# Strassen's algorithm for 28 of the 32 K tiles of each MLP's second product, with its sums on VectorE

## The chip, the core and the metric

One core of one Trainium2 chip runs the whole kernel. The metric is the device time of one execution in microseconds (us), as the median of several runs. The engines are TensorE (PE in the profile; PEld is its loading of the stationary operand), VectorE (DVE), ScalarE (ACT), GpSimd (POOL) and SyncE (SP), which only issues transfers here.

## The reference

A trunk of two layers works on 512 tokens of width 1024, in float32. Each layer has a token mixer (differential attention in layer 0, a short gated convolution in layer 1) and an MLP of width 4096, each between two RMS norms and added to the residual:

```python
def sq_relu_mlp(h, x, w_up, w_down):
    return jnp.square(jax.nn.relu(x @ w_up)) @ w_down

for i in range(DEPTH):                                   # DEPTH = 2
    h = rmsnorm(x, norm_mixer_pre[i])
    m = diff_attention(h, ...) if i % 2 == 0 else short_conv(h, ...)
    x = x + rmsnorm(m, norm_mixer_post[i])
    h = rmsnorm(x, norm_mlp_pre[i])
    x = x + rmsnorm(sq_relu_mlp(h, mlp_w_up[i], mlp_w_down[i]), norm_mlp_post[i])
```

The change concerns the product with `w_down`: [512 tokens, 4096] times [4096, 1024], in both layers.

## The kernel before

Every float32 operand is split into two parts, `hi` (rounded) and `lo` (the rest), and a product of two operands is three matmuls into one PSUM bank: `mm3`, lines 63 to 65. A bank holds 128 x 512 numbers.

**Weights.** A unit of weights is [128, 1024]: one K tile of `w_down` (`dn`) with all 1024 output columns, or one tile of 128 features of `w_up` (`up`) with its 8 K tiles. SP loads the raw unit (three buffers). ACT casts `hi` (line 143) and DVE subtracts to get `lo` (line 144), in `split_to`; `use` has the units split three ahead of the one in use, and 9 units have room as parts.

**The MLP.** `mlp_steps` says in which order groups of up tiles and groups of K tiles ("dn") follow each other. An up tile makes 128 hidden features for all 512 tokens: 24 matmuls of 512 columns into one bank (`feature_tiles`). The first six up tiles of a layer are an exception (`HALVED`): they go in two passes of 256 tokens, 24 matmuls of 256 columns per tile and pass, since the first tokens are normed and transposed before the last. ACT then takes relu and square out of the bank (lines 569, 570), and DVE makes the two parts of the activations, `u_hi` and `u_lo` (lines 572, 573).

`down(g)` multiplies a group of K tiles: groups of 4, 4, 4, 4, 4, 4 and 8. For each block of 128 tokens and each half of the output columns, the K tiles of the group run up in one bank, and DVE adds the bank into `acc` in SBUF (line 606; line 604 copies in the first group). The banks take turns over six. The four up tiles of a group lie between two such groups on PE. The last group of 8 goes by whole token blocks. Behind each block comes `block_end`: the post norm (`mg`, line 501; the mean square on ACT; the power -1/2 on POOL, line 70), the residual (`x_sb`, line 506), the next norm (`hn`, line 515). `turn` transposes `hn` on PE through banks 6 and 7 (line 523), and ACT and DVE take the parts out (`hT_hi`, line 526, `hT_lo`, line 527). It is put behind 18 further steps of PE (`after`, `step`); a step is one `mm3` of 512 columns. What comes next is the convolution's first product (`ci`), whose first tiles go in two passes of 256 tokens as well.

Each engine runs its instructions in order. The order is made once, when the program is built, by a scheduler that takes for each engine what its model thinks is ready.

Of the kernel before, what the change touches and what calls it, by code (L numbers as in the profile page):

```python
# [16 lines left out]
P = 128  # L17
T = 512
# [9 lines left out]
DOWN_GROUPS = (4, 4, 4, 4, 4, 4, 8)  # L28
MASKED = -3.0e38
SLOTS = 9  # L30
# [3 lines left out]
SHARERS = {2: {30, 31}, 4: {29}}  # units of attention that are last to use the banks  # L34
# [3 lines left out]
def trunk(ctx: ExitStack, tc: tile.TileContext, x, xT, w_qk, w_v, w_o, w_in, w_out,  # L38
# [6 lines left out]
    up_ = ctx.enter_context(tc.tile_pool(name="u", bufs=9))  # L45
# [41 lines left out]
    # ---- weights: units of [P, 1024] in the order of their use, loaded as slots fall free and  # L87
    # ---- split exactly into two parts of 12 bits some units ahead of their use
    starts = [sum(DOWN_GROUPS[:g]) for g in range(len(DOWN_GROUPS))]
    group = [list(range(s, s + n)) for s, n in zip(starts, DOWN_GROUPS)]  # L90
    conv_order = [8, 16, 0, 9, 17, 1] + [r * KT + ct for ct in range(2, KT) for r in (1, 2, 0)]
    order = [("v", k, w_v[k]) for k in range(KT)]
    order += [(n, h, w_qk[2 * h + i]) for h in range(H) for i, n in enumerate("qk")]
    order += [("wo", k, w_o[k]) for k in range(KT)]

    # the last group of K tiles goes through whole token blocks, the others through all tokens at once
    mlp_steps = [("up", 0)]
    for g in range(len(group) - 1):
# [12 lines left out]
    raws, units, xts = [], [], []
    n_done = [0]

    def issue():
        while len(raws) < min(len(order), len(units) + RAWS):
            n, i, src = order[len(raws)]
# [12 lines left out]
            raws.append(raw)  # L129
# [4 lines left out]
    def split_to(j):  # L134
        for j_ in range(len(units), min(j + 1, len(order), n_done[0] + SLOTS)):
            n, i, _ = order[j_]
            raw = raws[j_]
            if n == "v":
                split_xT(i)
            hi = wp.tile([P, 1024], F32R, tag="whi", name=f"hi_{n}_{i}")  # L140
            lo = wp.tile([P, 1024], F32R, tag="wlo", name=f"lo_{n}_{i}")
            for s in pieces(1024, j_ < 2 or n in "qk"):
                (DVE.tensor_copy if j_ < 1 else ACT.copy)(hi[:, s], raw[:, s])  # L143
                DVE.tensor_tensor(lo[:, s], raw[:, s], hi[:, s].bitcast(F32), op=ALU.subtract)  # L144
            units.append((hi, lo))
# [23 lines left out]
    def split_xT(kt):  # L169
        """x transposed (as laid out by the host), times the gain"""  # L170
# [14 lines left out]
    ones = const.tile([P, P], F32, name="ones")  # L185
# [6 lines left out]
    mask = const.tile([P, P], F32, name="mask")  # L192
# [73 lines left out]
    def rotate(i, which, h, p):  # L266
# [9 lines left out]
        def split_q(c, mine, other):  # L276
            """scaled: hi and lo of each component, where its rows are"""
# [4 lines left out]
        def twin_q(c, mine, other):  # L282
            """hi again, on the other half of the rows"""
# [432 lines left out]
```

## Time and profile before

| | |
|---|---|
| median of 3 runs | 1155.06 us (1154.93 to 1156.70) |
| profiled execution, first to last instruction (span) | 1153.8 us |
| PE busy | 1134.4 us, 98% of the span, 5584 matmuls |
| DVE busy | 632.9 us, 55% |
| ACT busy | 434.5 us, 38% |
| POOL busy | 100.3 us, 9% |

The profiled execution has no time of its own besides its span; the median of the runs is 1.3 us longer than that span. A busy share is a mean over the program, so the sections below look at stretches of it. The MLP of layer 0 lies at about 262 to 615 us, the convolution at 615 to 800, the MLP of layer 1 behind that.

### The profile page before, as it was taken

Reading aid. Unit: us, or ns where it says so; the run is one execution under the profiler, and the core shown is the slowest. Engines: PE = TensorE matmul, PEld = TensorE weight load, DVE = VectorE, ACT = ScalarE, POOL = GpSimd, SP = SyncE. Lnnn points to the kernel's source line nnn. Section 1 sums busy time; section 2 is a strip of 40 time slices with the busy share of each in tenths; the row PEclk is TensorE's granted clock in tenths of the full one; section 3 lists DMA queues with packets and bytes.
Section 4 is the critical chain, followed back from the end, with each engine's and each line's share of the span. In section 5 each row is a group of like instructions: output and inputs, shape, how many; then the busy total and the mean of one; then the engine's idle time right before and its main releaser. Section 6 shows DMA issues by size and latency. Waiting matters only on the chain.

```text
span 1153.8 us, 14203 instructions
## 1 busy us (share of the span) xinstructions
PE 1134.4 (98%) x5584; PEld 946.8 (82%) x5584; DVE 632.9 (55%) x1007; ACT 434.5 (38%) x789; POOL 100.3 (9%) x108
## 2 busy tenths in 40 slices
PE   9999999999999999999999999999999999999997
PEld 7867677779888888888889988889988888888886
DVE  6589999666543443544357544447544434434424
ACT  6546666544422322313324432225423223222411
POOL 0144454211000000000001000000000000000000
PEclk9999999999999999999999999999999999999999
DMA  8611111044431421423205323303414314313201
GB/s 317 217 59 52 56 56 55 19 152 153 134 103 43 146 99 48 146 74 128 92 1 183 129 91 99 102 19 130 144 37 146 106 40 146 100 46 130 89 19 55
DMA packets 33044, 114.32 MB, mean 99 GB/s; under 512 B 3793, under 2 KB 4433, under 8 KB 32977
## 3 DMA queue, kind: packets, MB, share of 16 engines
q1 hardware_dynamic: 32976, 113.41, 29.3%
q8 instruction: 44, 0.72, 0.3%
q14 instruction: 24, 0.19, 0.1%
HBM read 111.30 MB, written 2.10 MB: 98 GB/s over the span
## 4 chain that ended last, share of the span: by engine, by line
PE 83%; DVE 11%; POOL 3%; issue 2%; ACT 1%; DMA 0%; SPq 0%; POOLq 0%; DVEq 0%; ACTq 0%
PE bank L63 25%; PE bank L65 25%; PE bank L64 25%; PE pair L206 2%; PE bank L206 2%; DVE nm L372 1%; DVE a L397 1%; POOL t_q L272 1%; PE bank L523 1%; DVE k L289 1%; DVE pair L371 1%; PE pair L63 1%; PE pair L65 1%; PE pair L64 1%; DVE q L284 1%
## 5 line engine op out<-in xcount | busy, mean ns | idle before, releaser
L63 PE MATMUL bank<-hT_hi,hi_up 128*128 128x512 f32 (+1 forms) x608 | 216.5, 356 | 0.0
L64 PE MATMUL bank<-hT_lo,hi_up 128*128 128x512 f32 (+1 forms) x608 | 216.3, 356 | 0.0
L65 PE MATMUL bank<-hT_hi,lo_up 128*128 128x512 f32 (+1 forms) x608 | 216.2, 356 | 0.0
L63 PE MATMUL bank<-hi_dn,u_hi 128*128 128x512 f32 (+1 forms) x520 | 200.8, 386 | 0.0
L65 PE MATMUL bank<-hi_dn,u_lo 128*128 128x512 f32 (+1 forms) x520 | 200.6, 386 | 0.0
L64 PE MATMUL bank<-lo_dn,u_hi 128*128 128x512 f32 (+1 forms) x520 | 200.6, 386 | 0.0
L143 ACT CAST hi_dn<-raw_dn 128x1024 fp32r<-128x1024 f32 x64 | 65.8, 1053 | 245.8 <-PE bank L65 141.9
L606 DVE TENSOR_TENSOR acc<-bank,acc 128x512 f32<-128x512 f32 (+1 forms) x97 | 66.2, 684 | 149.5 <-PE bank L65 149.5
L144 DVE TENSOR_TENSOR lo_dn<-raw_dn,hi_dn 128x1024 fp32r<-128x1024 f32 x64 | 77.6, 1223 | 104.9 <-ACT hi_dn L143 104.9
L65 PEld LDWEIGHTS bank<-hT_hi,lo_up 128*128 128x128 f32 x608 | 114.7, 189 | 16.2
L64 PEld LDWEIGHTS bank<-hT_lo,hi_up 128*128 128x128 f32 x608 | 114.8, 189 | 16.2
L63 PEld LDWEIGHTS bank<-hT_hi,hi_up 128*128 128x128 f32 x608 | 114.7, 189 | 16.2
L143 ACT CAST hi_up<-raw_up 128x1024 fp32r<-128x1024 f32 x64 | 66.4, 1051 | 157.5 <-PE bank L65 65.9
L144 DVE TENSOR_TENSOR lo_up<-raw_up,hi_up 128x1024 fp32r<-128x1024 f32 x64 | 77.8, 1223 | 72.8 <-ACT hi_up L143 72.8
L63 PEld LDWEIGHTS bank<-hi_dn,u_hi 128*128 128x128 f32 x520 | 97.7, 188 | 19.7
L64 PEld LDWEIGHTS bank<-lo_dn,u_hi 128*128 128x128 f32 x520 | 97.7, 188 | 19.6
L65 PEld LDWEIGHTS bank<-hi_dn,u_lo 128*128 128x128 f32 x520 | 97.7, 188 | 19.6
L63 PE MATMUL bank<-hT_hi,hi_ci 128*128 128x512 f32 (+1 forms) x240 | 83.4, 347 | 0.0
L64 PE MATMUL bank<-hT_lo,hi_ci 128*128 128x512 f32 (+1 forms) x240 | 83.2, 347 | 0.0
L65 PE MATMUL bank<-hT_hi,lo_ci 128*128 128x512 f32 (+1 forms) x240 | 83.2, 347 | 0.0
L64 PEld LDWEIGHTS bank<-hT_lo,hi_ci 128*128 128x128 f32 x240 | 45.4, 189 | 5.7
L65 PEld LDWEIGHTS bank<-hT_hi,lo_ci 128*128 128x128 f32 x240 | 45.4, 189 | 5.7
(195 smaller groups left out, 1652.9 us busy)
## 6 DMA issues: line engine op xcount, KB each, us to landing
raw_up<-in_w_up SPq DMA_DIRECT2D x64, 512.0 KB, 3.5
raw_dn<-in_w_down SPq DMA_DIRECT2D x64, 512.0 KB, 3.5
raw_ci<-in_w_in SPq DMA_DIRECT2D x24, 512.0 KB, 3.4
raw_q<-in_w_qk SPq DMA_DIRECT2D x8, 512.0 KB, 4.3
raw_k<-in_w_qk SPq DMA_DIRECT2D x8, 512.0 KB, 4.3
raw_wo<-in_w_o SPq DMA_DIRECT2D x8, 512.0 KB, 3.5
raw_wc<-in_w_out SPq DMA_DIRECT2D x8, 512.0 KB, 3.4
raw_v<-in_w_v SPq DMA_DIRECT2D x7, 512.0 KB, 5.1
```

The source lines that it names most:

```text
L63: PE.matmul(o, lhsT=a[0], rhs=b[0], start=start, stop=False)
L64: PE.matmul(o, lhsT=a[0], rhs=b[1], start=False, stop=False)
L65: PE.matmul(o, lhsT=a[1], rhs=b[0], start=False, stop=stop)
L143: (DVE.tensor_copy if j_ < 1 else ACT.copy)(hi[:, s], raw[:, s])
L144: DVE.tensor_tensor(lo[:, s], raw[:, s], hi[:, s].bitcast(F32), op=ALU.subtract)
L206: PE.matmul(banks[2 * b + n], lhsT=hT[ai][:, kt, b * P:(b + 1) * P], rhs=w[bi][:, n * 512:(n + 1) * 512], start=kt == 0 and ai + bi == 0, ...
L272: POOL.tensor_tensor(t1, t1, sw, op=ALU.add)
L284: DVE.tensor_scalar(tiles[c][other], t1[mine], HD ** -0.5, None, op0=ALU.mult)
L289: DVE.tensor_tensor(tiles[c][other], t1[mine], tiles[c][mine].bitcast(F32), op=ALU.subtract)
L371: DVE.tensor_tensor(dgl, dgl, mask.unsqueeze(1).broadcast_to([P, 2, P]), op=ALU.add)
L372: DVE.tensor_reduce(nm, s[:, :, :w], axis=AX.X, op=ALU.max, negate=True)
L606: DVE.tensor_tensor(a, o, a, op=ALU.add)
```

## The change

28 of the 32 K tiles of each layer's second product go in 14 pairs. A pair is a 2 x 2 block problem: two K tiles by two halves of the tokens (256 each) on the side of the activations, two K tiles by two halves of the columns (512 each) on the side of the weights. Instead of the 8 products of such blocks there are 7, of sums of blocks. Two pairs make a group, so there are 7 groups per layer. A product of a group is 12 matmuls: two pairs by two token blocks by three.

- **Activations.** Relu and square of the two tiles of a pair go into one scratch tile `F` of eight blocks [128, 256], of which there is one buffer. DVE makes four sums of blocks in three instructions; `ua` (768 wide) and `ub` (1024 wide) are split into parts, `hi` now on ACT. The scratch of the norms (`jk`) and of the convolution uses `F` too.
- **Weights.** A pair's raw weights are one tile of five blocks of 512 (`rawd`, two buffers), and its units are `A` (1024, split as loaded), `E` (sums of 1024 and 512, then split), `D` (512 per pair) and `G` (a sum of 512, then split). Units are split four ahead, into 6 slots; in the other stages two more lie in the buffers of `rawd`.
- **Products.** X is banks 0 and 1, Y is 2 and 3, Z is 4 and 5. In order: X, Y, X again (it runs on in the same bank), Z, X, Z, X. After each of the seven DVE adds both banks into a quarter of `acc` (`into`); in the first group the first write of each quarter is an ACT copy. Up tiles behind the first six use banks 6 and 7 in turn.
- **Order.** Four up tiles lie between two groups, six before the last. The four K tiles that are left go by token blocks as before (`tail`); `turn` follows after 14 steps, and `mg` has two buffers instead of three.

```diff
-DOWN_GROUPS = (4, 4, 4, 4, 4, 4, 8)
-SLOTS = 9
+PAIRED = 28
+GROUP = 2
+SLOTS = 6
+LEAD = 4
+RAWDS = 2
...
+        else:
+            r, (h2, l2) = parts[0], (t.rearrange("p (a b) -> p a b", a=2) for t in (hi, lo))
+            if n[0] == "A":
+                split(h2, l2, r[:, 0:4:2, :])
+            if n[0] == "E":
+                DVE.tensor_tensor(r[:, 0:2, :], r[:, 0:2, :], r[:, 1:4:2, :], op=ALU.add)
+                DVE.tensor_tensor(r[:, 4, :], r[:, 0, :], r[:, 3, :], op=ALU.add)
+                split(h2, l2, r[:, 0:5:4, :])
+            if n[0] == "D":
+                for k, p in enumerate(parts):
+                    split(h2[:, k, :], l2[:, k, :], p[:, 3, :])
+            if n[0] == "G":
+                DVE.tensor_tensor(r[:, 2, :], r[:, 4, :], r[:, 2, :], op=ALU.add)
+                split(h2, l2, r[:, 1:3, :])
...
-            sq = t512(late, f"relu_{l}_{i}", "relu", 3)
-            ACT.activation(sq, o, AF.Relu)
-            ACT.activation(sq, sq, AF.Square)
-            u = u_tile(f"u_{l}_{i}")
-            DVE.tensor_copy(u[0], sq)
-            DVE.tensor_tensor(u[1], sq, u[0].bitcast(F32), op=ALU.subtract)
-            us[i] = u
...
+                held[p] = late.tile([P, 8, 256], F32, tag="F", name=f"F_{l}_{p}", bufs=1)
+            f = held[p]
+            squared(o.rearrange("p (a b) -> p a b", a=2), f[:, k:k + 3:2, :])
...
+            split(*a, f[:, 1:4, :])
+            DVE.tensor_tensor(f[:, 4:6, :], f[:, 1:3, :], f[:, 0:1, :].broadcast_to([P, 2, 256]), op=ALU.subtract)
+            DVE.scalar_tensor_tensor(f[:, 6, :], f[:, 4, :], -1.0, f[:, 2, :], op0=ALU.mult, op1=ALU.subtract)
+            DVE.scalar_tensor_tensor(f[:, 7, :], f[:, 6, :], -1.0, f[:, 3, :], op0=ALU.mult, op1=ALU.subtract)
+            split(*b, f[:, 4:8, :])
...
+        def product(g, o, first, form, kind, half):
+
+            for p in groups[g]:
+                w = use(f"{kind}{l}", p if kind != "D" else g)
+                s = half if kind != "D" else groups[g].index(p)
+                s = slice(512 * s, 512 * s + 512)
+                for t in range(2):
+                    step(lambda: mm3(o[t], part(us[form, p], ALL, slice(t * P, (t + 1) * P)), part(w, ALL, s),
+                                     first and p == groups[g][0], p == groups[g][-1], not first))
+
+        def into(c, o, op, fresh=False):
+
+            for t in range(2):
+                a = acc[:, (2 if c[0] == 1 else 0) + t, 512 * (c[1] - 1):512 * c[1]]
+                if fresh:
+                    ACT.activation(a, o[t], AF.Copy, scale=1.0 if op == ALU.add else -1.0)
+                else:
+                    DVE.tensor_tensor(a, a, o[t], op=op)
 
         def down(g):
...
+            x, y, z = ([banks[2 * i], banks[2 * i + 1]] for i in range(3))
+            new, pq = g == 0, groups[g]
+            product(g, x, True, "A11", "A", 0)
+            into((1, 1), x, ALU.add, new)
+            product(g, y, True, "A12", "A", 1)
+            into((1, 1), y, ALU.add)
...
+            product(g, x, False, "S2", "E", 1)
+            into((1, 2), x, ALU.subtract, new)
+            product(g, z, True, "S1", "E", 0)
+            into((2, 2), z, ALU.subtract, new)
...
+            product(g, x, False, "S3", "G", 0)
+            into((2, 2), x, ALU.subtract)
+            product(g, z, False, "S4", "D", 0)
+            into((1, 2), z, ALU.subtract)
+            done(f"D{l}", g)
+            product(g, x, False, "A22", "G", 1)
+            into((2, 1), x, ALU.add, new)
```

How the instructions stand on DVE before, in the second group of K tiles of layer 0 (`bank4` and `bank5` are banks that `down` has filled, `lo_dn0_9` is the second part of a unit that comes later):

```order
L573 TENSOR_TENSOR u_0_11_lo_3330<-relu_0_11_3326,u_0_11_hi_3329 128x512
L606 TENSOR_TENSOR acc_81<-bank4_2593,acc_81 128x512
L606 TENSOR_TENSOR acc_81<-bank5_2594,acc_81 128x512
...
L606 TENSOR_TENSOR acc_81<-bank4_2593,acc_81 128x512
L144 TENSOR_TENSOR lo_dn0_9_3536<-raw_dn0_9_3364,hi_dn0_9_3535 128x1024
L606 TENSOR_TENSOR acc_81<-bank5_2594,acc_81 128x512
L144 TENSOR_TENSOR lo_dn0_10_3573<-raw_dn0_10_3465,hi_dn0_10_3572 128x1024
```

And on DVE in the changed kernel, in the third group of layer 0 (pairs 4 and 5; `lo_G0_4` is the second part of unit G of pair 4, `ua_0_6` and `ub_0_6` are the activations of pair 6, which the next group uses; bank 0 at the end is the third product's):

```order
L201 TENSOR_TENSOR lo_G0_4_3578<-rawd_0_4_3329,hi_G0_4_3577 128x1024
L699 TENSOR_TENSOR F_0_6_3519<-F_0_6_3519 128x512
L724 TENSOR_TENSOR acc_81<-acc_81,bank0_70 128x512
L201 TENSOR_TENSOR ua_0_6_lo_3555<-F_0_6_3519,ua_0_6_hi_3554 128x768
L700 SCALAR_TENSOR_TENSOR F_0_6_3519<-F_0_6_3519 128x256
L724 TENSOR_TENSOR acc_81<-acc_81,bank1_71 128x512
L701 SCALAR_TENSOR_TENSOR F_0_6_3519<-F_0_6_3519 128x256
L724 TENSOR_TENSOR acc_81<-acc_81,bank2_2575 128x512
...
L201 TENSOR_TENSOR lo_G0_5_3605<-rawd_0_5_3332,hi_G0_5_3604 128x1024
L201 TENSOR_TENSOR ub_0_6_lo_3557<-F_0_6_3519,ub_0_6_hi_3556 128x1024
L201 TENSOR_TENSOR lo_up0_14_3616<-raw_up0_14_3361,hi_up0_14_3615 128x1024
L724 TENSOR_TENSOR acc_81<-acc_81,bank0_70 128x512
```

The adds of banks, which stood almost alone, now stand among sums and splits. Between the second product's add (bank 3, left out) and the third product's (bank 0) there are three splits of 1024.

On ACT at the same place of the changed kernel:

```order
L674 ACTIVATE F_0_6_3519<-bank6_72 128x2x256
L675 ACTIVATE F_0_6_3519<-F_0_6_3519 128x2x256
L200 CAST hi_G0_4_3577<-rawd_0_4_3329 128x1024
L674 ACTIVATE F_0_6_3519<-bank7_73 128x2x256
L675 ACTIVATE F_0_6_3519<-F_0_6_3519 128x2x256
L200 CAST ua_0_6_hi_3554<-F_0_6_3519 128x768
L200 CAST hi_G0_5_3604<-rawd_0_5_3332 128x1024
```

The cast of `hi_G0_4` needs a slot, and it stands ahead of the second tile's relu.

On DVE at the tail of layer 0 in the changed kernel, between the second and the third token block (`m0_1`, `m0_2`; banks 2 and 3 are block 2's, bank 4 is block 3's, banks 6 and 7 at the end hold the transposes of block 1):

```order
L621 SCALAR_TENSOR_TENSOR hn_m0_1_1_5071<-x_sb_2313,rb_m0_1_5066,g_pre2_2581 128x512
L768 TENSOR_TENSOR acc_81<-bank3_2576,acc_81 128x512
L607 TENSOR_TENSOR mg_m0_2_0_5111<-acc_81,g_post1_2579 128x512
L607 TENSOR_TENSOR mg_m0_2_1_5113<-acc_81,g_post1_2579 128x512
L601 TENSOR_SCALAR a_m0_2_0_5115<-a_m0_2_0_5115 128x1
L201 TENSOR_TENSOR lo_ci_17_5212<-raw_ci_17_4954,hi_ci_17_5211 128x1024
L73 TENSOR_SCALAR ra_m0_2_5122<-a_m0_2_1_5116,a_m0_2_0_5115 128x1
L768 TENSOR_TENSOR acc_81<-bank4_2577,acc_81 128x512
L612 SCALAR_TENSOR_TENSOR x_sb_2313<-mg_m0_2_0_5111,ra_m0_2_5122,x_sb_2313 128x512
L612 SCALAR_TENSOR_TENSOR x_sb_2313<-mg_m0_2_1_5113,ra_m0_2_5122,x_sb_2313 128x512
L633 TENSOR_TENSOR hT_lo_80<-bank6_72,hT_hi_79 128x4x128
```

The parts of block 1's transposes stand behind the residual of block 2, as before; new between them are a split of the convolution's weights and the first add of block 3.

## Rows read from the trace of the kernel before

**Rows 1.** The page, parts 1, 2 and 4: busy time, granted clock, chain

```profile
PE 1134.4 (98%) x5584; PEld 946.8 (82%) x5584; DVE 632.9 (55%) x1007; ACT 434.5 (38%) x789; POOL 100.3 (9%) x108
...
PEclk9999999999999999999999999999999999999999
...
PE 83%; DVE 11%; POOL 3%; issue 2%; ACT 1%; DMA 0%; SPq 0%; POOLq 0%; DVEq 0%; ACTq 0%
```

**Rows 2.** Windows: stretch, PE, PEld, DVE, ACT, POOL busy, granted clock, DMA share

```profile
230.00:262.00 32.00, 30.05 (x150) 24.71 (x149) 20.48 (x40) 15.28 (x35) 5.05 (x6) 1.00 0.46 153
...
288.00:420.00 132.00, 132.00 (x624) 111.00 (x623) 61.76 (x80) 42.22 (x55) 0.00 (x0) 1.00 0.30 96
...
570.00:615.00 45.00, 45.00 (x208) 37.41 (x207) 25.86 (x46) 16.16 (x35) 4.34 (x8) 1.00 0.08 26
```

**Rows 3.** Groups by form, PE: busy, mean ns of one, idle before

```profile
L63 PE MATMUL bank<-hi_dn,u_hi 128*128 128x512 f32 x504 | 196.2, 389 | 0.0
```

**Rows 4.** Timeline of PE: the second product, 24 matmuls from start to start

```profile
570.02 0.39 PE L63 MATMUL bank<-hi_dn,u_hi 128*128 128x512 f32 x1
...
575.46 0.39 PE L63 MATMUL bank<-hi_dn,u_hi 128*128 128x512 f32 x1
```

**Rows 5.** Timeline of PE: matmuls of 256 columns, start to start

```profile
290.07 0.28 PE L63 MATMUL bank<-hT_hi,hi_up 128*128 128x256 f32 x1
...
290.43 0.28 PE L63 MATMUL bank<-hT_hi,hi_up 128*128 128x256 f32 x1
```

**Rows 6.** Groups by form, DVE

```profile
L144 DVE TENSOR_TENSOR lo_dn<-raw_dn,hi_dn 128x1024 fp32r<-128x1024 f32 x64 | 77.6, 1223 | 104.9 <-ACT hi_dn L143 104.9
L606 DVE TENSOR_TENSOR acc<-bank,acc 128x512 f32<-128x512 f32 x95 | 65.4, 690 | 146.7 <-PE bank L65 146.7
L573 DVE TENSOR_TENSOR u_lo<-relu,u_hi 128x512 fp32r<-128x512 f32 x64 | 44.3, 693 | 2.2
L572 DVE CAST u_hi<-relu 128x512 fp32r<-128x512 f32 x64 | 27.4, 427 | 3.6 <-ACT relu L570 3.6
...
L397 DVE SCALAR_TENSOR_TENSOR a<-p,rho 128x256 f32<-128x256 f32 x8 | 3.8, 476 | 0.0
```

**Rows 7.** Timeline of DVE: instructions one behind the other

```profile
503.98 1.23 DVE L144 TENSOR_TENSOR lo_up<-raw_up,hi_up 128x1024 fp32r<-128x1024 f32 x1 [1.07 <-ACT hi_up L143]
505.12 0.68 DVE L606 TENSOR_TENSOR acc<-bank,acc 128x512 f32<-128x512 f32 x1
505.73 2.35 DVE L144 TENSOR_TENSOR lo_up<-raw_up,hi_up 128x1024 fp32r<-128x1024 f32 x2
```

**Rows 8.** Groups by form, ACT

```profile
L143 ACT CAST hi_dn<-raw_dn 128x1024 fp32r<-128x1024 f32 x64 | 65.8, 1053 | 245.8 <-PE bank L65 141.9 <-PE bank L64 85.6 <-DMA raw_dn<-in_w_down 18.3
L570 ACT ACTIVATE relu<-relu 128x512 f32<-128x512 f32 x64 | 40.6, 634 | 2.0
L569 ACT ACTIVATE relu<-bank 128x512 f32<-128x512 f32 x64 | 37.9, 592 | 3.5 <-PE bank L65 3.5
...
L288 ACT CAST k<-t_k 64x512 fp32r<-64x512 f32 x16 | 9.9, 618 | 16.7 <-POOL t_k L272 16.5
```

**Rows 9.** Timeline: last matmul of a bank and the add that waits for it

```profile
579.99 0.39 PE L65 MATMUL bank<-hi_dn,u_lo 128*128 128x512 f32 x1
...
580.41 1.37 DVE L606 TENSOR_TENSOR acc<-bank,acc 128x512 f32<-128x512 f32 x2 [7.03 <-PE bank L65]
```

**Rows 10.** Timeline of DVE: end of the first token block, layer 0

```profile
581.70 1.29 DVE L501 TENSOR_TENSOR mg_m<-acc,g_post 128x512 f32<-128x512 f32 x2
...
584.10 1.41 DVE L506 SCALAR_TENSOR_TENSOR x_sb<-mg_m,ra_m,x_sb 128x512 f32<-128x512 f32 x2 [0.73 <-POOL ra_m L70]
...
587.31 1.42 DVE L515 SCALAR_TENSOR_TENSOR hn_m<-x_sb,rb_m,g_pre 128x512 f32<-128x512 f32 x2 [0.73 <-POOL rb_m L70]
...
596.32 0.68 DVE L527 TENSOR_TENSOR hT_lo<-bank,hT_hi 128x512 fp32r<-128x512 f32 x1
```

**Rows 11.** Timeline of PE: the transposes of the first block

```profile
593.14 1.03 PE L523 MATMUL bank<-ident,hn_m 128*128 128x128 f32 x8
```

More of the change, by code (lines that the diff above doesn't have):

```diff
@@ L100, in trunk @@
-    mlp_steps += [("dn", len(group) - 1)]
-    def mlp_order(l):
-        src = {"up": w_up, "dn": w_down}
-        return [(f"{n}{l}", i, src[n][l, i]) for n, g in mlp_steps for i in group[g]]
+    order = [("v", k) for k in range(KT)]
+    order += [(n, h) for h in range(H) for n in "qk"]
+    order += [("wo", k) for k in range(KT)]
+    groups = [list(range(g, g + GROUP)) for g in range(0, PAIRED // 2, GROUP)]
+    rest = list(range(PAIRED, FT))
+    mlp_steps = [("first", list(range(HALVED)))]
@@ new lines, in trunk, with loaded_by @@
+    source = {"v": w_v, "wo": w_o, "ci": w_in, "wc": w_out}
+    for l in range(2):
+        source |= {f"up{l}": w_up[l], f"dn{l}": w_down[l]}
+    def loaded_by(u):
+        n, i = u
+        if n[0] in "AEG" and n[1:].isdigit():
+            return [("rawd", n[1], i)]
+        if n[0] == "D":
+            return [("rawd", n[1], p) for p in groups[i]]
+        return [("raw", n, i)]
+    loads, first_use, last_use = [], {}, {}
+    for j, u in enumerate(order):
+        for ld in loaded_by(u):
+            if ld not in last_use:
+                loads.append(ld)
+                first_use[ld] = j
+            last_use[ld] = j
@@ new lines, in trunk @@
+    units, raws, xts = [], {}, []
+    n_done = [0]
+    n_issued = [0]
+    in_flight = {"raw": [], "rawd": []}
+    limit = {"raw": RAWS, "rawd": RAWDS}
+    allowed = ["raw"]
+    beside = {u for u in order if u[0] in ("v", "q", "k", "wo", "ci", "wc")}
+    where, ring = [], {"w": [], "rawd": []}
+    for j in range(len(order)):
+        tag = "rawd" if order[j] in beside and j % (SLOTS + RAWDS) >= SLOTS else "w"
+        size = SLOTS if tag == "w" else RAWDS
+        where.append((tag, ring[tag][-size] if len(ring[tag]) >= size else -1))
+        ring[tag].append(j)
@@ new lines, in issue @@
+    def issue():
+        while n_issued[0] < len(loads):
+            ld = loads[n_issued[0]]
+            tag, n, i = ld
+            live = in_flight[tag] = [x for x in in_flight[tag] if last_use[x] >= len(units)]
+            if len(live) >= limit[tag] or tag not in allowed:
+                return
+            if tag == "rawd" and any(n_done[0] <= j < first_use[ld] for j in ring["rawd"]):
+                return
+            live.append(ld)
+            first = n_issued[0] == 0
+            n_issued[0] += 1
+            if tag == "rawd":
+                raw = raws[ld] = wp.tile([P, 5, 512], F32, tag=tag, name=f"rawd_{n}_{i}", bufs=RAWDS)
+                for k in range(2):
+                    nc.sync.dma_start(raw[:, 2 * k:2 * k + 2, :].rearrange("p a b -> p (a b)"), w_down[int(n), 2 * i + k])
+                continue
@@ L146, in split_to, with use @@
+        units.append((hi, lo))
+    def split_to(j):
+        for j_ in range(len(units), min(j + 1, len(order))):
+            if where[j_][1] >= n_done[0]:
+                break
+            make(j_)
             issue()
-    def use(n, i, lead=3):
+    def use(n, i, lead=LEAD):
         j = place[n, i]
@@ L184, in trunk @@
     issue()
[L185 removed]
+    ones = ap.tile([P, P], F32, name="ones", bufs=1)
     DVE.memset(ones, 1.0)
@@ L576, in up @@
-        def up(g):
-            if g == 0:
-                feature_tiles(f"up{l}", range(HALVED), finish, True)
-            for i in group[g]:
-                if i >= HALVED:
-                    feature_tiles(f"up{l}", [i], finish)
-        def down(g):
-            last = g == len(group) - 1
+            if i >= PAIRED:
+                f = late.tile([P, 8, 256], F32, tag="F", name=f"F_{l}_{i}", bufs=1)
+                sq = f[:, 0:2, :].rearrange("p a b -> p (a b)")
+                squared(o, sq)
+                us["plain", i] = u_tile(f"u_{l}_{i}", i)
+                split(*us["plain", i], sq)
+                return
@@ L625, in conv_finish @@
         if role == 1:
-            held["c"] = t512(late, f"c_{ct}", "relu", 3)
+            scratch = late.tile([P, 4, 512], F32, tag="F", name=f"conv_{ct}", bufs=1)
+            held["c"], held["y"], held["z"] = (scratch[:, k, :] for k in range(3))
             ACT.copy(held["c"], o)
```

176 lines of the change are left out of this document (112 added, 64 removed).

## The prediction

> **What bounds the kernel now.** I began with the page: TensorE is busy 98% of the span at the full granted clock, VectorE 55%, ScalarE 38%, and 83% of the chain that ended last is PE [rows 1]. The windows say the same of the stage that the change touches: in the middle of the first MLP (288 to 420 us) PE is busy all the time at clock 1.00, VectorE 47% and ScalarE 32% of it, and in the tail of that MLP (570 to 615 us) still 45.0 of 45.0 us [rows 2]. So a matmul taken away there is time, as long as the other engines keep up. What one costs is its pitch, not its 389 ns [rows 3], since matmuls overlap: 24 starts of 512 columns take 575.46 - 570.02 = 5.44 us, 0.227 us each [rows 4]; three of 256 columns take 0.36 us, 0.12 each [rows 5]. VectorE's adds of banks now wait for PE (146.7 us of idle time in front of 95 adds [rows 6]): VectorE is ahead.
>
> **What is saved.** Before, the second product takes 1512 matmuls of 512 columns (three lines of 504 [rows 3]) and 48 of 256. After, it is 14 groups of 7 x 12 = 84 matmuls, and 180 plus 24 halves in the two tails: 1356 and 24. That is 156 x 0.227 + 24 x 0.12 = 35.4 + 2.9 = **38.2 us**, if PE waits for nothing. The rest is the question whether VectorE, whose work grows, makes it wait.
>
> **VectorE's load.** A period of a middle group is four up tiles (96 matmuls, 21.8 us) and one group (84, 19.0 us): 40.8 us of PE. VectorE's instructions in it, by the rows of the same shapes [rows 6]: 1.22 us for 1024 columns, 0.69 for 512 whether from PSUM or SBUF, 0.48 for a scalar_tensor_tensor of 256, and for the split of 768, which no row shows, 0.96 (halfway between 512 and 1024; bounds 0.69 and 1.22).
> - splits of four up units: 4 x 1.22 = 4.9
> - two pairs of weights: A 1.22, E 1.22 + 0.69 + 1.22, D 0.69, G 0.69 + 1.22, 6.95 per pair: 13.9
> - two pairs of activations: 0.96 + 0.69 + 2 x 0.48 + 1.22 = 3.83 per pair: 7.7
> - 14 adds: 14 x 0.69 = 9.7
>
> Together 36.1 us, 88% of the period. But durations overstate it: one split of 1024 starts 1.14 us before the next instruction and an add 0.61 [rows 7], some 0.085 less than they last. With 42 instructions that is 3.6 less: 32.5 us, 80%. VectorE remains under PE's time by either count. ScalarE: four relus and squares 4.9, four up casts 4.2, 2 x 3 weight casts of 1.05 and 2 of 0.62, two pairs of activation casts of about 0.8 and 1.05: 20 us of 40.8 [rows 8], not a bound. Casting the activations on ScalarE takes 0.43 us a tile from VectorE [rows 6]; that is in the sum already.
>
> [...]
>
> **Where an average does not help: inside a group.** A product lasts 12 x 0.227 = 2.72 us, and banks 0 and 1 serve four of the seven products: the first, third, fifth and seventh. The fifth starts on bank 0 at 10.9 us after the group's start, plus one matmul of an up tile that stands ahead: 11.1. By then VectorE must have added the third product out of bank 0, in the order of its row: G's first split, the difference, add, ua's split, a sum, add, a sum, two adds, G's second split, ub's split, an up split, then this add. G's first cast gets its slot when the last up tile ends (0.16 us into the group), ScalarE takes 1.05 [rows 8], so VectorE begins at 1.28. Bank waits on the way cost it nothing: a bank can be read 0.42 us after its last matmul's start [rows 9], at 2.2 and 2.9 for the first product, and VectorE comes to those two at 3.0 and 4.9. By start-to-start times it reaches the add in question at 10.5 and ends at 11.2, 0.1 us late; by full durations 1.1 late. Later adds fit: the fifth product's are done at about 16.5, the seventh starts at 16.6. VectorE ends the group's work 0.8 us into the next up phase, which has some 4 us to spare since its splits wait for slots that up tiles free at 10.9, 16.3 and 21.8. I take **0.3 us** for each of 6 groups in 2 layers, **3.6 us**; bounds 0.1 x 12 = 1.2 and 1.1 x 12 = 13.2.
>
> **First groups.** Here six up tiles end within 17.3 us (second passes of 24 x 0.12 = 2.88 us), and the one buffer of F chains the pairs: second relu and square 1.23, ua's cast 0.8 and split 0.96, difference 0.69, two sums 0.96, ub's cast 1.05 and split 1.22, 6.9 us per pair if nothing comes between [rows 6, 8], against 5.76 us of PE; A, E, D and G of two pairs want VectorE in the same stretch. Following the row orders, ua of the second pair is ready at 20.5 and its ub at 23.3 us after the start of the second passes; PE, reordered for that, ends the group at 39.8 instead of 37.9. That is 2 us, **4 us** for both layers; bounds 0 and one whole chain, 6.9, each.
>
> **Tail of layer 0.** Blocks now end every 24 x 0.227 = 5.44 us instead of 10.9. VectorE's part of a block's end is two adds 1.37, mg 1.29, residual 1.41, hn 1.42, two hT_lo of 0.68, some 0.7 of small ones: 7.6 by durations, 7 by starts, with two waits of 0.73 for POOL in it [rows 9, 10]. It falls behind. The convolution's first pass needs blocks 0 and 1 turned. Counted from the last group's start, PE has done the four blocks at 40.8 and wants that at 43.4; VectorE makes hn of block 1 by 40.6, just as PE comes to its transposes, which before came 12.7 us behind the block's first add [rows 9, 11]; but hT_lo of block 1 stands behind block 2's residual and an add of block 3, and ends at 46.5. **3.3 us**, with 0 and 6 as bounds (block 2's chain before it, or behind it and one more wait). In layer 1 nothing follows a block but its output, and the chain behind the last matmul keeps its length: 0.
>
> **Priced at nothing.** Pair loads are two transfers per pair, into buffers that come free when the group has made G, 8 us into it, 25 us before their next use. The one buffer of F in norms and convolution serves ScalarE's own sequence or a tile every 16.3 us.
>
> **Sum.** 38.2 - 3.6 - 4 - 3.3 = 27.3 us less. The profiled span of 1153.8 becomes 1126.5, the median of 1155.06, 1.3 above its span, about **1128 us**.
>
> [...] The rows show 1.00 in a stretch with 2 us of PE idle [rows 2], so waits this short are priced at their length.
>
> **Rivals.**
> 1. *VectorE by full durations.* It is 88% loaded, each group waits 1.1 us: 13.2, the first groups 4 each, the tail 6: 27 lost, 11 gained, **1144** (1136 to 1150). For it: the order crowds sums and splits ahead of the adds; I costed one group by hand, and others may stand worse. [...] Against: the starts [rows 7].
> 2. *VectorE keeps up entirely*, as the middle groups almost allow: no loss, **1117** (to 1118).
> 3. *The in-place adds cost more, and it is slower.* If an add from PSUM among dependent sums took 1.3 us, the five ahead of the fifth product would add 5 x 0.6 to the 0.3: 3.3 x 12 + 7.3 = 47 lost, **1164**. It decides from 1.15 us per add, where each group waits 2.6. Against: 690 ns for an add of the same operands, 95 times [rows 6].
>
> **Chances.** 0.66 for my forecast (1118 to 1136), 0.20 for the first rival, 0.06 for the second, 0.08 for something worse, of which 0.05 lies above 1157. The range reaches from no loss, 1117, to the first rival's centre and a little over, 1146; all upper bounds together (13.2 + 13.8 + 6) would give 1150. A difference of 0.2% (2.3 us) is about what a measurement of this kernel can tell. All cases but the slow one are faster: 0.93, within it 0.02, slower 0.05.
>
> **What would show it.** The count of PE matmuls falls by 180, with the pitch in middle groups unchanged. VectorE's share in the middle of an MLP rises from 47% to 80 to 88%. PE's waits should stand at three places: before the fifth product on bank 0 (released by an add of a bank, tenths of a us), in each layer's first group, and before the convolution's first tiles (released by hT_lo). The prediction is wrong if PE waits for VectorE in every product, if VectorE's instructions in the sums last longer than their shapes' rows, or if the waits are on ScalarE or a transfer.

## The result, and the profile after

The changed kernel takes 1127.14 us (median of 4 runs, 1126.57 to 1129.97), against 1155.88 beside it on the same chips: a ratio of 0.9758 with a 95% interval from 0.9741 to 0.9774. It is faster by 2.4%, 0.9 us under the forecast of 1128. The profiled execution has a span of 1125.9 us, 27.9 less than before.

The page of the changed kernel, parts 1, 2 and 4, answers to [rows 1]:

```profile
PE 1101.4 (98%) x5404; PEld 915.7 (81%) x5404; DVE 823.4 (73%) x1251; ACT 545.2 (48%) x925; POOL 99.0 (9%) x108
...
PEclk9999999999999999999998999999999999999999
...
PE 80%; DVE 13%; POOL 3%; issue 2%; ACT 1%; DMA 1%; SPq 0%; POOLq 0%; DVEq 0%; ACTq 0%
```

180 matmuls are gone (5584 to 5404), PE is still busy 98%, and one slice has a granted clock under 0.9, where no slice had one. The windows (stretch, PE, PEld, DVE, ACT, POOL busy, granted clock) answer to [rows 2]:

```profile
288.00:420.00 132.00, 132.00 (x623) 110.17 (x622) 108.65 (x138) 73.72 (x97) 0.00 (x0) 1.00 0.28 96
...
570.00:615.00 45.00, 42.32 (x221) 36.05 (x220) 37.81 (x66) 23.42 (x47) 4.86 (x10) 0.92 0.32 108
```

In the middle of the MLP PE is busy throughout, as before, and VectorE went from 47% to 82% of the stretch. In the tail of layer 0 PE is idle 2.7 us and the clock is 0.92 on the mean; both were 0 and 1.00.

The groups by form of VectorE (busy, mean ns | idle before) answer to [rows 6]:

```profile
L724 DVE TENSOR_TENSOR acc<-acc,bank 128x512 f32<-128x512 f32 x180 | 116.5, 679 | 4.4 <-PE bank L69 4.4
...
L222 DVE TENSOR_TENSOR rawd<-rawd 128x1024 f32<-128x1024 f32 x28 | 33.5, 1218 | 0.2
L201 DVE TENSOR_TENSOR ua_lo<-F,ua_hi 128x768 fp32r<-128x768 f32 x28 | 26.6, 950 | 0.0
...
L700 DVE SCALAR_TENSOR_TENSOR F<-F 128x256 f32<-128x256 f32 x28 | 11.8, 421 | 0.4
...
L201 DVE TENSOR_TENSOR lo_G<-rawd,hi_G 128x1024 fp32r<-128x1024 f32 x28 | 34.2, 1220 | 44.2 <-ACT hi_G L200 44.2
```

The new instructions last what rows of their size had said: an add 679 ns, a sum of 1024 1218, the split of 768 950 (taken: 960), a sum of 256 421 (taken: 480). The adds of banks now wait 4.4 us for PE in all, where they had waited 146.7. VectorE still waits for ScalarE's casts in front of the splits of weights (44.2 us ahead of those of G).

**Where the time went.** Four points of PE's timeline, the same in both kernels, show where time was won and lost. The 84 matmuls that a layer's seven groups no longer need are worth 19.05 us at PE's pitch. From layer 0's first up matmul (260.75 before, 261.46 after) to the convolution's first 512-wide one (651.64, 641.35) the change wins 11.0 us of these 19.05: 8.05 are lost there. From layer 1's first up matmul (794.89, 784.60) to the last matmul (1146.92, 1118.24) it wins 18.4 of the 19.2 that are saved in that layer. The stretch behind the last matmul grew from 6.9 to 7.7, and layer 0's MLP begins 0.7 later, behind a stage that the change hardly touches (in two more traces of the changed kernel, below, it begins at 261.47 and 263.32, so this term varies from run to run). The saving of 38.2 less 8.05, 0.8, 0.8 and 0.7 is 27.9. So 10.3 us are lost, where 10.9 were forecast, but not in the forecast shares.

**Middle groups: nothing lost.** The third group of layer 0 begins at 381.01. VectorE there (start, duration):

```profile
382.07 1.23 DVE L201 TENSOR_TENSOR lo_G<-rawd,hi_G 128x1024 fp32r<-128x1024 f32 x1 [3.82 <-ACT hi_G L200]
383.22 0.69 DVE L699 TENSOR_TENSOR F<-F 128x512 f32<-128x512 f32 x1
383.83 0.68 DVE L724 TENSOR_TENSOR acc<-acc,bank 128x512 f32<-128x512 f32 x1
...
390.04 1.22 DVE L201 TENSOR_TENSOR lo_up<-raw_up,hi_up 128x1024 fp32r<-128x1024 f32 x1
391.17 2.47 DVE L724 TENSOR_TENSOR acc<-acc,bank 128x512 f32<-128x512 f32 x4
```

and PE at its fifth product:

```profile
391.66 0.39 PE L69 MATMUL bank<-hi_E,ub_lo 128*128 128x512 f32 x1
391.89 0.39 PE L67 MATMUL bank<-hT_hi,hi_up 128*128 128x512 f32 x1
392.12 0.40 PE L67 MATMUL bank<-hi_G,ub_hi 128*128 128x512 f32 x1
```

The add in question is the first of the four at 391.17. It ends at 391.85, 10.84 us into the group (the prediction's count had 11.2), and PE wants bank 0 at 392.12, 11.11 in: 0.27 us of room. All ten groups from the second to the sixth of both layers show the same to 0.02 us, and from one such group to the next PE takes 40.82 to 40.85 us, which is 180 matmuls at 0.227.

**The tail of layer 0: 7.3 us lost.** This is the 8.05 less some 0.75 for the layer's first group. PE there (the last matmul of the tail, then the convolution's first tiles):

```profile
598.27 0.40 PE L69 MATMUL bank<-hi_dn,u_lo 128*128 128x512 f32 x1
599.44 0.39 PE L67 MATMUL bank<-hT_hi,hi_ci 128*128 128x256 f32 x1 [0.77 <-ACT hT_hi L632]
...
599.90 0.81 PE L67 MATMUL bank<-hT_hi,hi_ci 128*128 128x256 f32 x2
602.47 0.58 PE L68 MATMUL bank<-hT_lo,hi_ci 128*128 128x256 f32 x1 [1.76 <-DVE b_m L601]
602.85 0.41 PE L69 MATMUL bank<-hT_hi,lo_ci 128*128 128x256 f32 x1
603.06 0.41 PE L67 MATMUL bank<-hT_hi,hi_ci 128*128 128x256 f32 x1
```

VectorE at the same time:

```profile
598.33 1.21 DVE L201 TENSOR_TENSOR lo_ci<-raw_ci,hi_ci 128x1024 fp32r<-128x1024 f32 x1
...
600.40 1.42 DVE L612 SCALAR_TENSOR_TENSOR x_sb<-mg_m,ra_m,x_sb 128x512 f32<-128x512 f32 x2
601.73 0.68 DVE L633 TENSOR_TENSOR hT_lo<-bank,hT_hi 128x512 fp32r<-128x512 f32 x1
602.33 0.14 DVE L601 TENSOR_SCALAR b_m<-b_m 128x1 f32<-128x1 f32 x1
602.39 0.68 DVE L633 TENSOR_TENSOR hT_lo<-bank,hT_hi 128x512 fp32r<-128x512 f32 x1
```

and the windows of that place:

```profile
600.00:601.00 1.00, 0.57 (x3) 0.19 (x1) 0.87 (x2) 0.00 (x0) 0.36 (x1) 1.00 0.39 86
601.00:602.00 1.00, 0.00 (x0) 0.00 (x0) 1.00 (x3) 0.72 (x2) 0.00 (x0) 0.65 0.92 324
602.00:604.00 2.00, 1.53 (x7) 1.53 (x8) 1.87 (x6) 1.58 (x3) 0.55 (x1) 0.50 0.15 57
...
606.00:608.00 2.00, 2.00 (x12) 2.00 (x11) 1.86 (x4) 0.00 (x0) 0.00 (x0) 0.50 0.04 18
608.00:609.00 1.00, 1.00 (x10) 1.00 (x9) 0.00 (x0) 0.00 (x0) 0.55 (x1) 0.94 0.87 356
```

PE starts 0.94 and then 2.33 us later than its pitch allows, 3.3 us together, the second time for the first hT_lo of block 1, which runs behind block 2's residual. (The row names the small instruction behind it, which came last before PE moved on.) And the granted clock falls to 0.50 in the wait, and stays there while PE is busy again: 27 matmuls of 256 columns start 0.21 us apart instead of 0.12, which is 2.5 us more. The rest of the 7.3 lies around the transposes, with a wait of 0.58 before those of block 3. (In the two other traces the tail takes 66.1 and 66.2 us from its first matmul to the convolution's first 512-wide one, where it takes 67.1 here, so the loss there is about 6.3.)

### The profile page after: what moved, and what is told of

It is laid out like the page before. It is cut to its first block, busy times and chain, and to the rows that moved or that the text cites. A ratio compares the mean times of both kernels' runs of the same rounds, so it can differ in the third digit from the quotient of the medians.

```text
span 1125.9 us, 14245 instructions
## 1 busy us (share of the span) xinstructions
PE 1101.4 (98%) x5404; PEld 915.7 (81%) x5404; DVE 823.4 (73%) x1251; ACT 545.2 (48%) x925; POOL 99.0 (9%) x108
## 4 chain that ended last, share of the span: by engine, by line
PE 80%; DVE 13%; POOL 3%; issue 2%; ACT 1%; DMA 1%; SPq 0%; POOLq 0%; DVEq 0%; ACTq 0%
PE bank L69 24%; PE bank L67 24%; PE bank L68 24%; PE bank L309 2%; PE pair L309 2%; DVE nm L475 2%; DVE a L500 1%; POOL t_q L375 1%; DVE k L392 1%; DVE x_sb L612 1%; DVE pair L474 1%; PE bank L629 1%; PE pair L67 1%; PE pair L69 1%; PE pair L68 1%
## 5 line engine op out<-in xcount | busy, mean ns | idle before, releaser
L724 DVE TENSOR_TENSOR acc<-acc,bank 128x512 f32<-128x512 f32 x180 | 116.5, 679 | 4.4 <-PE bank L69 4.4
L201 DVE TENSOR_TENSOR lo_G<-rawd,hi_G 128x1024 fp32r<-128x1024 f32 x28 | 34.2, 1220 | 44.2 <-ACT hi_G L200 44.2
L674 ACT ACTIVATE F<-bank 128x512 f32<-128x512 f32 x64 | 37.6, 593 | 45.3 <-PE bank L69 35.8
L200 ACT CAST hi_G<-rawd 128x1024 fp32r<-128x1024 f32 x28 | 29.5, 1053 | 46.0 <-PE bank L68 30.8
L201 DVE TENSOR_TENSOR lo_E<-rawd,hi_E 128x1024 fp32r<-128x1024 f32 x28 | 34.2, 1220 | 23.4 <-ACT hi_E L200 23.4
L201 DVE TENSOR_TENSOR lo_A<-rawd,hi_A 128x1024 fp32r<-128x1024 f32 x28 | 33.5, 1219 | 19.5 <-ACT hi_A L200 19.5
L200 ACT CAST hi_A<-rawd 128x1024 fp32r<-128x1024 f32 x28 | 29.5, 1053 | 30.4 <-PE bank L68 21.7
L67 PE MATMUL bank<-hi_A,ua_hi 128*128 128x512 f32 x112 | 44.0, 393 | 0.0
L68 PE MATMUL bank<-lo_A,ua_hi 128*128 128x512 f32 x112 | 43.6, 390 | 0.0
L67 PE MATMUL bank<-hi_E,ub_hi 128*128 128x512 f32 x112 | 43.6, 389 | 0.0
```

What stands on the lines that cost most here:

```text
L67: PE.matmul(o, lhsT=a[0], rhs=b[0], start=start, stop=False, skip_group_check=more)
L68: PE.matmul(o, lhsT=a[0], rhs=b[1], start=False, stop=False, skip_group_check=more)
L200: (DVE.tensor_copy if on_dve else ACT.copy)(hi, src)
L201: DVE.tensor_tensor(lo, src, hi.bitcast(F32), op=ALU.subtract)
L674: ACT.activation(dst, o, AF.Relu)
L724: DVE.tensor_tensor(a, a, o[t], op=op)
```

## The experiments

There were ten runs: seven edited kernels, one of them run twice, and the changed kernel twice more. The changed kernel's ratio to the kernel before was 0.9758, 0.9753 and 0.9759 in its three measurements, with intervals of about 0.0015 to either side, so a ratio that differs by 0.001 or less says nothing.

### Is there spare time in the middle groups?

Both kernels add to `down`, behind the second product's adds, instructions on VectorE whose result nobody reads: one in the first kernel (shown), three in the other (`range(3)`).

```diff
             into((1, 1), y, ALU.add)
+            for k in range(1):
+                DVE.tensor_reduce(small(f"extra_{l}_{g}_{k}"), y[1], axis=AX.X, op=ALU.max)
```

> One more VectorE instruction per group (a maximum over bank 3, 512 wide, written to a column that nobody reads), behind the second product's adds. In the changed kernel the add that frees bank 0 for the fifth product ends 10.85 us after a middle group's start and PE comes to bank 0 at 11.11: 0.26 us of room, in all ten middle groups (second to sixth of both layers). Theory (what counts is the place in VectorE's order): the instruction shifts the add by about 0.61, PE waits 0.35 us in each of ten groups, 3.5 us in all, about 1130.6 us. Rival (VectorE has 12 to 20% to spare in a period and catches up): no change, 1127 us.

Measured: 1126.27 us (1125.90 to 1126.89), ratio 0.9744 (0.9731 to 0.9758): no wait, so the theory's 3.5 us did not come.

> Three such instructions at the same place. Theory: 3 x 0.61 - 0.26 = 1.57 us of wait per middle group, 15.7 us in all, about 1143 us, and more if the granted clock falls behind waits of this length. Rival (spare time on average): VectorE's load rises by 1.8 us of a period of 40.8, still under 93%, so no change, 1127 us.

Measured: 1129.47 us (1128.93 to 1131.52), ratio 0.9775 (0.9759 to 0.9790): about 2 us more, not 16. The expectations had nothing on what the builder's scheduler does. With one more instruction, the four adds begin 10.76 us into a middle group, 0.6 later, but PE has four matmuls of the next up tile ahead of the fifth product where it had one, and comes to bank 0 at 11.78. With three there are seven, and PE comes at 12.90. In that kernel the room runs out at another place:

```profile
396.55 0.39 PE L68 MATMUL bank<-hT_lo,hi_up 128*128 128x512 f32 x1
397.08 0.50 PE L69 MATMUL bank<-hT_hi,lo_up 128*128 128x512 f32 x1
...
397.89 0.40 PE L67 MATMUL bank<-hi_G,ub_hi 128*128 128x512 f32 x1
```

PE's up matmul at 397.08 waits 0.3 us for its own weights' second part, whose split VectorE does at 395.81, right ahead of the adds at 396.94. The period of a middle group is 41.26 us instead of 40.82, 0.44 for 1.8 us of added work. So the 0.27 us of room in the changed kernel is no accident: with one, four and seven up matmuls ahead, PE comes to the bank 0.27 to 0.35 us behind the add in all three kernels, as if the scheduler put in as many as the add needs. The 2 us lie in layer 1 (335.7 us from its first up matmul to the last matmul, 333.6 in the changed kernel). Layer 0 as a whole gave nothing away in this kernel, since its tail came out 3 to 4 us shorter.

### Is it the wait that slows the matmuls behind it?

This kernel puts 24 matmuls that nobody reads ahead of the convolution's first tiles:

```diff
+        if halves and name == "ci":
+            w = use(name, tiles[0])
+            for _ in range(24):
+                PE.matmul(os[0][:, 0:256], lhsT=w[0][:, 0:P], rhs=w[0][:, P:P + 256], start=True, stop=True)
         for cut in cuts:
```

> 24 matmuls of 256 columns that nobody reads, ahead of the convolution's first tiles in PE's order, where PE waits 0.94 and 2.33 us for the transposed block 1. Theory: the 25 slow matmuls behind that wait (0.213 instead of 0.12 us apart, granted clock 0.50) come from the wait; with PE busy in it the clock stays at 1.00 and some 2.3 us are saved, about 1125 us, although the wait itself is only filled. Rival (those matmuls are slow for another reason, such as the convolution's operands or the transfers beside them): the slow stretch stays, no change, or up to 3 us longer for the added matmuls.

Measured: 1128.51 us (1127.32 to 1128.87), ratio 0.9761 (0.9747 to 0.9776). The windows of that place:

```profile
600.00:602.00 2.00, 2.00 (x19) 2.00 (x18) 1.87 (x5) 0.63 (x3) 0.55 (x1) 1.00 0.32 57
602.00:604.00 2.00, 1.18 (x10) 0.97 (x10) 2.00 (x6) 1.53 (x5) 0.00 (x0) 1.00 0.51 205
604.00:606.00 2.00, 2.00 (x19) 2.00 (x18) 1.87 (x4) 1.97 (x4) 0.55 (x1) 1.00 0.00 0
```

The clock stays at 1.00, so the low clock did come from the wait and not from the convolution's operands. But no time was won. The added matmuls still leave 0.98 us of wait for hT_lo, which ends as long behind the tail's start as before (28.2 us for the first), and PE comes to the transposes of block 3 too early and starts them 1.23 us late (0.58 before). The stage from the tail's first matmul to the convolution's first 512-wide one takes 66.0 us, as in two of three traces of the changed kernel (below). This does not show that the low clock costs nothing. The edit also moved those transposes in PE's order: 84 of the convolution's matmuls stand ahead of the last of them instead of 92, and the other eight, 1.0 us, come behind. The first half of block 3's norm was ready 40.3 us behind the tail's start, against 42.4, 41.3 and 41.4 in the changed kernel, so that chain did get faster. What the held clock is worth alone stays open.

### Is it VectorE's load in the tail?

Here the products with the post norm's gain go from VectorE to GpSimd in layer 0:

```diff
-            DVE.tensor_tensor(m, p, g_post[:, c], op=ALU.mult)
+            (POOL if name[:2] == "m0" else DVE).tensor_tensor(m, p, g_post[:, c], op=ALU.mult)
```

> In the tail of layer 0 the two products with the post norm's gain (mg, 2 x 0.61 us per block on VectorE) go to GpSimd. Theory (VectorE's backlog of some 7 us per block against 5.44 makes the wait): block 1's second part (hT_lo) comes some 2.4 us earlier, the wait of 3.3 us shrinks to about 1 and the clock does not fall behind it: 4 to 5 us less, about 1122.5 us. Rival (the chain of each block, not VectorE's load, sets it): GpSimd takes about 1.29 us per product in this trace, 2.6 us for the two, so the residual and the next norm come no earlier or some 0.5 us later, and the time stays or grows by a us.

Measured: 1132.28 us (1130.49 to 1134.25), ratio 0.9796 (0.9779 to 0.9813): 4 to 5 us slower than the changed kernel, worse than either expectation. VectorE's and GpSimd's rows (VectorE first):

```profile
590.21 2.45 DVE L621 SCALAR_TENSOR_TENSOR hn_m<-x_sb,rb_m,g_pre 128x512 f32<-128x512 f32 x2 [1.10 <-POOL acc L791]
...
600.66 1.95 DVE L201 TENSOR_TENSOR lo_ci<-raw_ci,hi_ci 128x1024 fp32r<-128x1024 f32 x1
...
602.59 2.22 DVE L201 TENSOR_TENSOR lo_ci<-raw_ci,hi_ci 128x1024 fp32r<-128x1024 f32 x1
```

```profile
590.17 1.27 POOL L607 TENSOR_TENSOR mg_m<-acc,g_post 128x512 f32<-128x512 f32 x1
...
600.22 3.51 POOL L607 TENSOR_TENSOR mg_m<-acc,g_post 128x512 f32<-128x512 f32 x2 [3.32 <-DVE acc L768]
```

Beside GpSimd's multiplication a split of 1024 takes 1.95 to 2.22 us instead of 1.22, and the two instructions of a norm 2.45 instead of 1.41. GpSimd's own take 1.75 each beside the splits, and 1.27 where the norm runs beside one. So this run says nothing on the load. The next kernel leaves those products out and hands the residual the product without the gain:

```diff
-            DVE.tensor_tensor(m, p, g_post[:, c], op=ALU.mult)
+            if name[:2] == "m0":
+                m = p
+            else:
+                DVE.tensor_tensor(m, p, g_post[:, c], op=ALU.mult)
```

> Leaves out a part of the computation: the post norm's gain in the four blocks of layer 0's MLP (two VectorE instructions of 0.61 us a block), with nothing given to GpSimd. Theory (load on VectorE): with 1.2 us a block less, block 1's hT_lo comes some 2.5 us earlier although it still stands behind block 2's residual, PE waits under 1 us, the clock holds: 1122 to 1124 us. This is what moving them to GpSimd was to give; if it comes out so, the 5 us that the move cost instead came from GpSimd's side (its instructions last 1.3 to 1.75 us and VectorE's beside them up to 2.2 for 1.2). Rival (the chain of one block, through ScalarE and GpSimd's power, sets it and not the load): no more than 1 us less.

Measured: 1127.76 us (1125.39 to 1130.18), ratio 0.9755 (0.9736 to 0.9774): no change, and not the 1122 to 1124 us of the theory of the load. VectorE in this kernel:

```profile
599.69 1.22 DVE L201 TENSOR_TENSOR lo_ci<-raw_ci,hi_ci 128x1024 fp32r<-128x1024 f32 x1
...
600.97 1.23 DVE L201 TENSOR_TENSOR lo_ci<-raw_ci,hi_ci 128x1024 fp32r<-128x1024 f32 x1
...
603.05 1.42 DVE L615 SCALAR_TENSOR_TENSOR x_sb<-acc,ra_m,x_sb 128x512 f32<-128x512 f32 x2 [0.73 <-POOL ra_m L74]
604.38 0.69 DVE L636 TENSOR_TENSOR hT_lo<-bank,hT_hi 128x512 fp32r<-128x512 f32 x1
```

The time set free was given to one more split of the convolution's weights (two stand there where one stood), and hT_lo of block 1 still stands behind block 2's residual, which waits 0.73 us for GpSimd's power. VectorE reaches it as long after the tail's start as before (the second hT_lo ends 28.7 us behind it, in the changed kernel 28.8). So the work ahead of hT_lo did not become less, and a lighter load as such was not tested: what the run shows is that taking instructions away does not help as long as the order stays.

### Is it the order?

The next kernel makes a block's transposes due 8 steps behind it, not 14:

```diff
-                block_end(f"m{l}_{b}", b, [acc[:, b, c] for c in cuts], g_post, g_next, 14, last=l == 1, cuts=cuts)
+                block_end(f"m{l}_{b}", b, [acc[:, b, c] for c in cuts], g_post, g_next, 8, last=l == 1, cuts=cuts)
```

> The transposes of a block in the tail of layer 0 are due 8 steps behind its end instead of 14. That moves them 4 to 6 matmuls ahead in PE's order, and on VectorE it puts both hT_lo of block 1 ahead of block 2's residual and the first add of block 3, no longer behind them. Theory (the wait is made by what stands ahead of hT_lo of block 1 in VectorE's order, and the slow clock behind it by the wait): hT_lo of block 1 ends about 599.5 instead of 603.1, PE's wait there falls from 3.3 to under 1 us and no matmul runs at the lower clock; the stretch from the tail's first matmul to the convolution's first 512-wide one falls from 67.1 to about 62 us, the whole by 4 to 5, about 1122.5 us. Rival (VectorE has too much to do in the tail whatever the order; what is put first delays the rest): PE waits instead for the norm of block 1 at its transposes, or for blocks 2 and 3 later on, by as much, 1126 to 1128 us.

Measured: 1124.87 us (1124.23 to 1126.48), ratio 0.9731 (0.9718 to 0.9745); in the second setting, below, 1125.57. That is 2.6 and 2.8 us under the changed kernel. The runs of the two kernels do not overlap in either setting. The clock in the tail is 1.00, and hT_lo of block 1, now ahead of block 2's residual in VectorE's order, ends 26.1 us behind the tail's start, 2.7 earlier. Half of the rival holds too. PE waits for the norms at the transposes instead (part of the list of PE's waits: total us, times, longest):

```profile
PE bank L629 <- DVE hn_m L621: 3.2, 4, 1.3
```

> The changed kernel as it is, beside the two others on one chip. All theories: 1127 us, with the slow stretch behind the wait for hT_lo of block 1 as before.

Measured beside the kernels without the gain and with the earlier transposes: 1127.46 us (1126.56 to 1128.71), ratio 0.9753 (0.9740 to 0.9767).

### Is it that the blocks end too quickly?

Here layer 0 has six groups of pairs and eight K tiles in its tail; its last four up tiles lie behind the sixth group. Not shown below: the units of that tail may lie in two more buffers than the changed kernel's, so the edit changes more than the distance of the blocks.

```diff
-PAIRED = 28
+PAIRED = 24, 28
...
-                block_end(f"m{l}_{b}", b, [acc[:, b, c] for c in cuts], g_post, g_next, 14, last=l == 1, cuts=cuts)
+                block_end(f"m{l}_{b}", b, [acc[:, b, c] for c in cuts], g_post, g_next, 18 if l == 0 else 14, last=l == 1, cuts=cuts)
```

> Layer 0 keeps 8 K tiles for the token blocks at its end (24 of 32 in pairs, six groups, transposes 18 steps behind a block, as before the change); layer 1 stays as changed. That gives back 12 matmuls of 512 columns, 2.7 us. Theory (blocks that end every 5.44 us are too quick for the chain on VectorE, by its order and by what it has to do; at 10.9 us they are not): no wait and no lower clock in that tail, 6.2 to 7.2 us gained there, so 3.5 to 4.5 net, 1123 to 1124 us, a little under the kernel with the earlier transposes. Rival (the loss lies in the stage behind, the convolution's first weights and the turned blocks, whatever the tail): only the 2.7 us are added, 1130 us.

Measured: 1124.15 us (1123.40 to 1125.42), ratio 0.9727 (0.9713 to 0.9740). The windows of its tail:

```profile
560.00:600.00 40.00, 40.00 (x186) 33.28 (x185) 22.58 (x43) 13.45 (x31) 4.34 (x8) 1.00 0.08 26
600.00:620.00 20.00, 20.00 (x164) 19.73 (x163) 14.92 (x22) 9.89 (x17) 1.94 (x2) 1.00 0.74 235
```

PE waits nowhere in it, and the clock stays at 1.00. Paying back 12 matmuls (2.7 us) wins 4.3 against the changed kernel of the same setting, as the theory had it. It is the fastest of all, though its lead of 1.4 us over the one with earlier transposes is no more than the spread of the runs.

> The kernel with the transposes due 8 steps behind a block, once more beside the one with 8 K tiles at the end. All theories: 1125 us, PE waiting for the norms at the transposes, the granted clock at 1.00 in the tail.

Measured: 1125.57 us (1124.94 to 1127.01), ratio 0.9738 (0.9725 to 0.9751).

> The changed kernel on the same chip as the two before. All theories: 1127 us; the length of the stretch at the lower clock shows how much it varies from run to run (2.5 us given away in the first trace, 1.7 in the second).

Measured: 1128.41 us (1127.04 to 1128.79), ratio 0.9759 (0.9745 to 0.9772). In the three traces of the changed kernel 27, 18 and 14 matmuls run at the lower clock (the lowest stretch of 2 us in each shows 0.50, 0.50 and 0.54), which costs 2.5, 1.7 and 1.3 us; the wait in front of them is 3.3 each time.

## Why the prediction came out

The time was right to 1 us. That PE is the bound and that the removed matmuls are worth 38.2 us at their pitch held: a middle group with its up tiles takes 40.82 us for 180 matmuls, and the saving less the losses found on PE's timeline is the measured gain. That VectorE's new instructions last what rows of their size say held, and so did the start-to-start count: 82% of the middle stretch by the page's busy time, no wait of PE in it, against the first rival's 1.1 us per group. The starts in the trace of the changed kernel agree: a subtraction of 0.69 us has the next instruction 0.61 behind its start (383.22 to 383.83). The losses were right in their sum (10.9 forecast, 10.3 measured) by errors that cancel, so that the total came within 1 us is in part luck:

- *Middle groups*: 3.6 forecast, 0 measured, below the stated lower bound of 1.2. The step "0.1 us late by start-to-start times" was off by almost 0.4, since VectorE began 0.2 earlier (1.06 instead of 1.28 us into the group) and the sums of 256 were shorter. I then took 0.3, further from the truth. What the prediction lacked altogether is what the first two experiments showed: the up matmul ahead of the fifth product, which I had counted, is put there by the builder, and more come when the add comes later.
- *First groups*: 4 forecast, 1.1 to 1.5 measured (0.57 and 0.5 of late starts in them, and 0.7 to 0.8 a layer by PE's timeline: 41.51 us from the first group to the second, 40.82 between later ones). The chain through F is as forecast: ub of the second pair is ready some 23 us behind the second passes' start, at 303.95. But PE's new order covers most of it: the second pair's share of the first products comes later, and two and five up matmuls stand between the later ones.
- *Tail of layer 0*: 3.3 forecast, 7.3 measured (6.3 in two more traces), above the bound of 6. The wait itself was right in place and size: 0.94 + 2.33 us, for hT_lo of block 1 behind block 2's residual. The failed step is "waits this short are priced at their length": the clock fell to 0.50, and the matmuls behind the wait took 2.5 us more (1.7 and 1.3). A second step failed beside it: no loss was priced behind that wait, and 1.5 us lie around the transposes. How far the two depend on each other is open: the kernel that held the clock won nothing, but it moved block 3's transposes too. The row on which the first of these steps rested, 2 us of PE idle at clock 1.00 [rows 2], was a sum of shorter waits in one execution (1.3 us at most, with work between), and no sign of what 3.3 us would do with five matmuls in them. In that same stretch, between 244 and 252 us, the clock fell in three of the later traces (below). In the changed kernel's first trace it was 0.50 in the wait and for 27 matmuls behind it, so my reading of that row was wrong.
- *End of layer 1*: 0 forecast, 0.8 measured. The last block's adds queue behind block 2's residual: its first add starts at 1117.30, when PE had been done with that bank since about 1115.7.

The cause given for the tail needs a correction as well. I argued with VectorE's load, 7 us per block against 5.44. Taking 1.2 us per block away changed nothing, though the scheduler then put other work in its place; making the transposes due earlier, which moves hT_lo of block 1 ahead of block 2's residual, or giving the blocks 10.9 us, did. It is the order, in which a block that is needed late stands ahead of one that is needed now, that makes this wait. That the short distance of the blocks is what lets the scheduler mix them is argued and not shown. How order and load share the rest (3.9 us of waits remain with the better order) is not settled.

## What to carry to other kernels

Cost a chain inside a stage by starts, not by durations (0.61 us against 0.69 for the subtraction above), and look at what the scheduler has put in front of a wait before pricing it: filler work there grows with the need. Where a product is made shorter, look at what follows it at each end: blocks that now finish twice as fast can bring more waiting than the product gave back, and it can pay to leave the last part of the work unimproved. Behind TensorE's waits of 0.94 and 2.33 us here the matmuls took 2.5 us more, at a clock of 0.50. So do not price such a wait by its length alone: look in its rows whether the clock fell behind it, in more than one execution, and ask whether the next wait would take back what a held clock gives.

## What the hardware showed that I had not expected

- The granted clock was 0.50 for 6.8 us in the changed kernel's first trace, from within the second of two waits, 0.94 and 2.33 us with five short matmuls between, and 27, 18 and 14 matmuls ran at the lower clock in three executions. Waits of 1.43, 0.6, 0.61 and 1.17 us spread over 27 us, in the kernel with earlier transposes, left it at 1.00.
- Layer 0's attention output lies ahead of what the edits change. PE is idle there once ahead of a transpose, between 244 and 250 us, and for how long differs from trace to trace. The clock fell behind it in the traces with an idle time of 2.37, 2.65 and 2.83 us (`e5_turn_8`, `e2_three_more`, `e6_no_mg`: 0.79, 0.87 and 0.79 on the mean of 244 to 252 us). It stayed at 1.00 with 2.29 and 2.03 us (`e4_mg_on_pool`, `e9_turn_8_again`) and in the others with 0.99 to 1.47. `e5_turn_8` and `e9_turn_8_again` are two runs of one kernel.
- In `e4_mg_on_pool` instructions of VectorE and GpSimd took longer where they ran at the same time: splits of 1024 1.95 to 2.22 us instead of 1.22, GpSimd's products 1.75 instead of 1.27. In two cases where one pair can be told apart, the instruction that began first kept its length: GpSimd's product at 590.17 took 1.27 us and VectorE's norm from 590.21 took 2.45 instead of 1.41, while a split at 612.08 took 1.21 and GpSimd's product from 612.24 took 2.19. What makes them longer is not shown.
